# Causal mask by GpSimd's index selection, second-half rotation on GpSimd, and three changes of order, in a two-layer transformer kernel

## The chip, the cores and the metric

The kernel runs on one NeuronCore of a Trainium2 chip. The core has a matrix engine (TensorE, PE in the profile, with its weight loads as PEld), three engines for elementwise work (VectorE or DVE, ScalarE or ACT, GpSimd or POOL) and a queue that only issues transfers (SyncE, SP). Each engine takes its instructions in a fixed order and waits on semaphores that the others raise. The metric is the device time of one execution in microseconds, as the median of several runs.

## The reference

Two layers over 1024 tokens of width 1024, in fp32. Layer 0 mixes tokens by attention in a window of 128 tokens with 16 query heads, 4 key heads and one sink logit a head; layer 1 mixes them by a gated linear recurrence (HGRN2). Each mixer is followed by an MLP with a squared ReLU and 4096 hidden units, and a norm ends it.

```python
def sliding_window_attention(h, positions, w_qkv, b_qkv, sinks, w_o):
    qkv = h @ w_qkv + b_qkv
    q, k = apply_partial_rotary(q, cos, sin), apply_partial_rotary(k, cos, sin)
    scores = einsum(q, band(k)) * HEAD_DIM ** -0.5        # own block of 128 keys and the one before
    mask = (delta >= 0) & (delta < WINDOW) & (key_pos >= 0)
    m = maximum(max(scores), sink); e = exp(where(mask, scores, NEG_INF) - m)
    probs = e / (sum(e) + exp(sink - m))
    return einsum(probs, band(v)) @ w_o
...
for layer in range(DEPTH):
    x = x + mixer(rmsnorm(x, mix_norm[layer]))
    x = x + square(relu(rmsnorm(x, mlp_norm[layer]) @ w_up)) @ w_down
return rmsnorm(x, final_norm)
```

## The kernel before

**How it is written.** The Python code emits operations in program order into a list (`Schedule.add`); a planner then decides, before the kernel is built, which engine runs each one and in what order. Every operation carries a cost in ns for each engine that may run it. `due` (from L146 on) walks the list with a clock that only TensorE's costs advance and gives each operation a due time; an operation emitted with a `lead` is ranked 120 ns earlier for each unit of it. `order` then plays the list through: at each engine's next free moment it takes the ready operation of the lowest rank. All instructions are issued from one line, L372, so the profile is told apart by the tiles' names and not by lines. A cost in the code is therefore not a time: a wrong one moves instructions.

**Numbers in two parts.** Large products run in fp32r, with each operand split into a high and a low part (`wh`, `wl` for weights, two tiles `a` for the other side), and three matmuls of 512 columns stand for one exact one. The splits are made by DVE and ACT.

**Tiles.** `a` are 58 long-lived tiles of 128x512, `t` 20 short-lived ones, `m` 7 for the attention's scores and weight sums, `wr` raw weights as they land, `q` and `p` four banks each of the accumulation memory, `sm` small columns, `c` constants, `d` tiles put by in DRAM.

**Attention** (`attention`). Tokens come in two halves of four blocks of 128. `qkv` of half 0 projects keys and values (column group 0) and two groups of query columns; `projected` adds the bias on DVE and calls `rope`, which rotates 16 of each head's 64 columns with four small DVE operations: two products with the tables of cosine and sine (tiles `c`), one difference, one sum. Then the attention of half 0 is interleaved with the projections of half 1, and the attention of half 1 with the output projection of half 0. The norm's factor `r` of half 1 is asked for at the first step of its projections.

For each key head and block, `attend_block` makes the scores on PE (two `q` banks), copies and masks them into a tile `m` (ACT, DVE), takes the maximum with the sink (DVE; the sink's column is written by POOL), the exponentials (ACT), divides (DVE, `m<-m,sm`) and transposes on PE. A trick folds the window: `m` holds own and previous keys in the same 128 columns, since exactly one of the two is inside the window. ACT copies the transposed weights to `y`; a DVE product of `y` with a mask of zeros and ones (`own`, `t<-t,c` in the profile) keeps those of own keys. `values` then multiplies `y` with the previous block's values and `own` with the difference of the two (PE, `q<-t,a`, 64 columns wide), for two blocks at a time. The first block has no predecessor and takes its mask from the accumulation memory.

**MLP.** The first half works by a Strassen-like scheme on pairs of 128 hidden units (`pair`, m from 0 to 15): seven products of 12 matmuls, named 1 to 7, in three banks. Products 1, 6, 7 and 4 run on in the same bank `main`, and after each of the first three ACT copies the running sum (`read`), before the next product of that bank may begin. Products 5 and 3 share `side`, 2 has `own`. After the last pair comes `down`, the second half of the MLP.

**The recurrence** (`recurrence`) multiplies small pieces, 64 rows by 32 or 64 columns, in true fp32; each is entered to the planner with a cost of `width * 2.06 / 2.4 + 3` ns (L1276). They are interleaved with the projections of other heads.

Of the kernel before, what the change touches and what calls it, by code (L numbers as in the profile page):

```python
# [15 lines left out]
ALU = mybir.AluOpType  # L16
AX = mybir.AxisListType

P = 128
# [6 lines left out]
MT = FF // P  # L26
# [292 lines left out]
class Net:  # L319
# [323 lines left out]
    def pair(self, m, x):  # L643

        w = self.strassen_weights(*(self.io["up"][self.layer, i] for i in (m, m + MT // 2)))

        def read(ps):
            z = self.t()
            self.take(z, ps)
            return z  # L650

        main, side, own = self.psum("q"), self.psum("q"), self.psum()
        self.product(main, w[1], x[1], True)
        u1 = read(main)
        self.product(own, w[2], x[2], True)
        self.product(side, w[5], x[5], True)
        p5 = read(side)
        self.product(main, w[6], x[6], False)
        u2 = read(main)
        self.product(side, w[3], x[3], False)  # L660
        self.product(main, w[7], x[7], False)
        u3 = read(main)
        self.product(main, w[4], x[4], False)
        def kept(name, z):
            self.hid[name, m] = self.keep(z)

        self.add_bank(u1, own)
        h00 = self.square_relu(u1)
        kept(1, h00)
        self.add_bank(u2, side)  # L670
        h01, t5, t6, t4 = self.square_relu(u2), *(self.t() for _ in range(3))
        self.tt("any", t5, h01, h00, ALU.subtract)
        kept(5, t5)
        self.tt("any", p5, p5, u3, ALU.add)
        h11 = self.square_relu(p5)
        kept(3, h11)
        self.tt("any", t6, h11, t5, ALU.subtract)
        kept(6, t6)
        self.tt("any", h01, h11, h01, ALU.subtract)
        kept(7, h01)  # L680
        h10 = self.square_relu(main, True)
        kept(2, h10)
        self.tt("any", t4, h10, t6, ALU.subtract)
        kept(4, t4)
# [188 lines left out]
        self.neg = self.const((P, 1))  # L873
        self.memset(self.neg, NEG)

    def rope(self, x, heads, n):
        half = ROT // 2
        v = x.rearrange("p (h d) -> p h d", d=HD)[:, :, :ROT].rearrange("p h (a r) -> p h a r", a=2)
        prod = []
        for tab in self.trig:  # L880
            y = self.t(F32, (P, 8, 2, half))[:, :heads]
            tb = tab[:, n].unsqueeze(1).unsqueeze(1).to_broadcast([P, heads, 2, half])
            self.tt("any", y, v, tb, ALU.mult, heads * ROT)
            prod.append(y)
        yc, ys = prod
        self.tt("any", v[:, :, 0], yc[:, :, 0], ys[:, :, 1], ALU.subtract, heads * half)
        self.tt("any", v[:, :, 1], yc[:, :, 1], ys[:, :, 0], ALU.add, heads * half)

    def k_tiles(self, i):
        if self.ks[i] is None:  # L890
# [34 lines left out]
    def projected(self, cg, n, ps, r):  # L925
        if cg == 0:
            self.keys_values(n, ps, r)
        else:
            q = self.a()
            self.stt(halves(q), straight(ps), r, halves(self.bias[cg]), ALU.mult, ALU.add)  # L930
            self.rope(q, 8, n)
            self.q[n][cg - 1] = q

    def keys_values(self, n, ps, r):
        W = NG * HD
        k, ps = self.t(F32, (P, W)), straight(ps)
        self.stt(k, ps[:, 0], r, self.bias[0][:, :W], ALU.mult, ALU.add, W)
        if n % 2 == 0:
            self.v.append(self.a(F32, (P, 2, W)))
        v = self.v[n // 2][:, n % 2].only(n)  # L940
        self.stt(v, ps[:, 1], r, self.bias[0][:, W:], ALU.mult, ALU.add, W)
        if n % 2 == 0:
            self.dv.append(self.a(F32, (P, 2, W)))
        if n:
            before = self.v[(n - 1) // 2][:, (n - 1) % 2].only(n - 1)
            self.tt("any", self.dv[n // 2][:, n % 2].only(n), v, before, ALU.subtract, W)
        self.rope(k, NG, n)
        pk = self.psum("q")[:, : 2 * P].rearrange("p (g s) -> p g s", g=2)
        for gp in range(2):
            self.transpose(pk[:, gp], k[:, gp * P : gp * P + P])  # L950
        for i, (first, end) in enumerate(K_SPANS):
            if not first <= n < end:
                continue
            ks, kl = self.k_tiles(i)
            c = slice((n - first) * P, (n - first) * P + P)
            for g in range(NG):
                r, o = self.rows(g)
                src, dst = pk[r, g // 2], ks[g][r, c].only(n)
                self.copy(dst, src, P)
                self.ts("Pool", ks[g][o, c].only(n), dst, 1.0, None, ALU.mult, None, P)  # L960
                self.tt("DVE", kl[g][r, c].only(n), src, dst.bitcast(F32), ALU.subtract, P)
# [41 lines left out]
    def attend_block(self, g, n, stacks):  # L1003
        i = (n >= 3) + (n >= 6)
        c = slice((n - 1 - K_SPANS[i][0]) * P, (n + 1 - K_SPANS[i][0]) * P)
        tok = slice((n % BPH) * P, (n % BPH) * P + P)
        ks, kl = self.ks[i][g].only(n - 1, n), self.kl[i][g].only(n - 1, n, "o")
        m = self.t(F32, (P, 4, P + 2), "m")
        self.ts("Pool", m[:, :, P : P + 1], self.sink[:, 4 * g : 4 * g + 4].unsqueeze(2), 1.0, None, ALU.mult, None, 4)
        scores = [self.psum("q").rearrange("p (h s) -> p h s", h=2) for _ in range(2)]  # L1010
        for h in range(4):
            self.mm(scores[h // 2][:, h % 2], stacks[h][:, tok], turned(ks[:, c]), h % 2 == 0, False, 2 * P)
        for h in range(4):
            self.mm(scores[h // 2][:, h % 2], stacks[h][:, tok], turned(kl[:, c]), False, h % 2 == 1, 2 * P)
        for jj, ps in enumerate(scores):
            mj = m[:, 2 * jj : 2 * jj + 2, :P].only(jj)
            ps = ps.rearrange("p h (s a) -> p h a s", a=2)
            self.copy(mj, ps[:, :, 1], 2 * P)
            prev = ps[:, :, 0] if n else self.neg.unsqueeze(2).to_broadcast([P, 2, P])
            mask = self.prev_mask.unsqueeze(1).to_broadcast([P, 2, P])  # L1020
            self.op("DVE", self.nc.vector.copy_predicated, [mj], [mask, prev], 70 + 2 * P * 1.04, mj, mask, prev)
        mx, den = self.t(F32, (P, 4), "sm"), self.t(F32, (P, 4), "sm")
        self.op("DVE", self.nc.vector.tensor_reduce, [mx], [m], 610, mx, m[:, :, : P + 1], AX.X, ALU.max, negate=True)
        for j in range(4):
            mj = m[:, j, : P + 1].only(f"e{j}")
            self.act(mj, mj, AF.Exp, P, bias=mx[:, j : j + 1], accum=den[:, j : j + 1].only(j))
        self.op("DVE", self.nc.vector.reciprocal, [den], [den], 100, den, den)
        self.tt("any", m[:, :, :P], m[:, :, :P], den.unsqueeze(2).to_broadcast([P, 4, P]), ALU.mult)
        pt = self.psum("q").rearrange("p (h s) -> p h s", h=4)
        for j in range(4):  # L1030
            self.transpose(pt[:, j], m[:, j, :P])
        own, v = self.t(F32, (P, 4, P)), self.v[n // 2].only(n)[:, n % 2, g * HD : g * HD + HD]
        mask = self.own_t.unsqueeze(1).to_broadcast([P, 4, P])
        if n:
            y = self.t(F32, (P, 4, P))
            self.copy(y, pt)
            self.tt("any", own, y, mask, ALU.mult)
            parts = [(y, self.v[(n - 1) // 2].only(n - 1)[:, (n - 1) % 2, g * HD : g * HD + HD]),
                     (own, self.dv[n // 2].only(n)[:, n % 2, g * HD : g * HD + HD])]
        else:  # L1040
            self.tt("DVE", own, pt, mask, ALU.mult)
            parts = [(own, v)]
        return parts
# [15 lines left out]
    def attention(self, layer):  # L1059
# [6 lines left out]
        run(self.qkv(0, *h[0]))  # L1066
        self.load_x([1])
        h.append(self.scaled(layer, 1))
        interleave(self.attend(0, out[0]), self.qkv(1, *h[1]), 16, 24)
        interleave(self.attend(1, out[1]), self.o_proj(0, out[0]), 24, 8)  # L1070
        self.mlp_first(layer)
# [173 lines left out]
    def recurrence(self, e, ready, totals, out):  # L1245
# [23 lines left out]
        def products(part, operands, late, width=CH // 2):  # L1269
            part = part.rearrange("p (c t) -> p c t", c=NC)  # L1270
            for hf, (k, qs) in enumerate(operands):
                for c in range(BPH):
                    for b in range(2):
                        rows = slice(b * CH, b * CH + CH)
                        j = 2 * c + b
                        self.mm(part[rows, hf * BPH + c], chunk(k, j), qs[j], True, True, width, 2.06, "columns", late)  # L1276

        def merge(part, lg):
            H = 1 << lg
# [295 lines left out]
```

## Time and profile before

| | |
|---|---|
| median of 3 runs | 2010.9 us (2010.59 to 2011.6) |
| the profiled execution's own time | 2007.87 us |
| its span, from the first to the last instruction | 2005.5 us |
| granted TensorE clock, mean | 0.998 |
| DVE busy | 1699.2 us, 85% |
| ACT busy | 1013.7 us, 51% |
| POOL busy | 62.7 us, 3%, in 124 instructions |
| moved by DMA | 345.88 MB, mean 172 GB/s |

The page's first part gives each engine's busy time, the second the busy share in 40 slices of the span, the fourth the chain of work that ended last, the fifth the costliest groups of instructions. In the prediction's rows, "us engine line op out<-in" is followed by the tile's size and a count; a bracket at the end of a row of the timeline says how long the engine had been idle and what ended that. A row of the windows gives, for a stretch, its length, then busy time and count of PE, PEld, DVE, ACT and POOL, the clock, the DMA share and GB/s. Matmuls are pipelined: one of 128x512 is shown as 0.38 us long, though the next may start after 0.22.

### The profile page before, as it was taken

To read this page: it belongs to the slowest core of one execution; us is meant where nothing else is said; L and a number is where in the kernel's file an instruction comes from. 1 tells how busy PE (TensorE), PEld (TensorE's weight loads), DVE (VectorE), ACT (ScalarE), POOL (GpSimd) and SP (SyncE) were. 2 spreads that over 40 slices of the span, in tenths; PEclk is the share of its full clock that TensorE was granted. 3 is DMA by queue.
4 is the path that set the end of the run, shared out by engine and by line. 5 is a ranking of instruction groups with operands and counts; after the bars stand their busy time and mean duration, and the time that the engine had idled before them with its cause. 6 is when DMAs were issued, how large, how long until landed. Compare 5 with 4: busy or idle time off the path is not lost.

```text
span 2005.5 us, 32701 instructions
## 1 busy us (share of the span) xinstructions
PE 1979.5 (99%) x11404; PEld 1718.5 (86%) x11404; DVE 1699.2 (85%) x3360; ACT 1013.7 (51%) x2045; POOL 62.7 (3%) x124
## 2 busy tenths in 40 slices
PE   9999999999999999999999999999999999999998
PEld 8877788888888888888888888888888888888887
DVE  8999899777778878799898999989977777887787
ACT  6567796554454323255345555554654445323352
POOL 4030100000000000000000000000000000000001
PEclk9999999999999999999999999999999999999999
DMA  6212463544468967745422212667444446886752
GB/s 216 90 53 59 127 222 120 184 167 160 146 204 292 314 217 264 235 163 176 146 63 78 78 59 90 207 208 244 142 167 160 146 162 237 286 301 215 236 179 85
DMA packets 196677, 345.88 MB, mean 172 GB/s; under 512 B 21536, under 2 KB 31776, under 8 KB 196512
## 3 DMA queue, kind: packets, MB, share of 16 engines
q1 hardware_dynamic: 195936, 343.28, 52.0%
q8 instruction: 89, 1.46, 0.3%
q14 instruction: 76, 0.62, 0.1%
q10 hardware_dynamic: 576, 0.52, 0.1%
HBM read 250.39 MB, written 93.32 MB: 171 GB/s over the span
## 4 chain that ended last, share of the span: by engine, by line
PE 85%; DVE 7%; DMA 3%; issue 2%; ACT 2%; POOL 0%; SPq 0%; POOLq 0%; DVEq 0%; ACTq 0%
PE q L372 51%; PE p L372 34%; DVE t L372 3%; DVE a L372 2%; DVE wl L372 1%; ACT t L372 1%; ACT a L372 1%; DMA wr<-in_down 1%; DVE m L372 0%; DMA a<-in_x 0%; ACT wh L372 0%; ACT m L372 0%; DMA t<-d 0%; DMA wr<-in_wqkv 0%; DMA wr<-in_wv 0%
## 5 line engine op out<-in xcount | busy, mean ns | idle before, releaser
L372 PE MATMUL q<-a,wh 128*128 128x512 f32 x2560 | 761.8, 379 | 3.5 <-ACT t L372 3.5
L372 PE MATMUL p<-a,wh 128*128 128x512 f32 x2112 | 644.6, 383 | 0.1
L372 PEld LDWEIGHTS q<-a,wh 128*128 128x128 f32 x2560 | 482.3, 189 | 74.1 <-ACT t L372 5.0
L372 PE MATMUL q<-a,wl 128*128 128x512 f32 x1280 | 484.9, 379 | 0.0
L372 PEld LDWEIGHTS p<-a,wh 128*128 128x128 f32 x2112 | 394.2, 189 | 54.6 <-issue 1.2
L372 PE MATMUL p<-a,wl 128*128 128x512 f32 x1056 | 401.6, 381 | 0.0
L372 ACT CAST a<-t 128x512 fp32r<-128x512 f32 x283 | 172.0, 619 | 286.0 <-PE q L372 142.8
L372 PEld LDWEIGHTS q<-a,wl 128*128 128x128 f32 x1280 | 241.9, 189 | 34.3
L372 ACT ACTIVATE t<-t 128x512 f32<-128x512 f32 x272 | 171.1, 631 | 189.8 <-DVE t L372 182.2
L372 DVE TENSOR_TENSOR wl<-wr,wh 128x512 fp32r<-128x512 f32 x352 | 240.6, 686 | 11.7 <-ACT wh L372 3.9
L372 DVE TENSOR_TENSOR t<-t,t 128x512 f32<-128x512 f32 (+3 forms) x364 | 224.9, 638 | 26.8 <-ACT t L372 23.1
L372 PEld LDWEIGHTS p<-a,wl 128*128 128x128 f32 x1056 | 199.7, 189 | 26.8 <-issue 0.4
L372 DVE TENSOR_TENSOR a<-t,a 128x512 fp32r<-128x512 f32 (+1 forms) x326 | 217.2, 685 | 6.4 <-ACT a L372 6.0
L372 DVE TENSOR_TENSOR wl<-m,wh 128x512 fp32r<-128x512 f32 x248 | 170.5, 689 | 16.7 <-ACT wh L372 10.1
L372 ACT COPY t<-q 128x512 f32<-128x512 f32 (+2 forms) x214 | 119.4, 560 | 112.6 <-PE q L372 111.5
L372 ACT CAST wh<-wr 128x512 fp32r<-128x512 f32 x173 | 106.5, 618 | 100.2 <-PE p L372 45.7
L372 DVE TENSOR_TENSOR m<-wr,wr 128x512 f32<-128x512 f32 x160 | 110.0, 689 | 39.7 <-DMA wr<-in_down 24.0
L372 DVE CAST wh<-wr 128x512 fp32r<-128x512 f32 x179 | 76.5, 427 | 78.9 <-PE q L372 47.2
L372 ACT CAST wh<-m 128x512 fp32r<-128x512 f32 x154 | 94.8, 618 | 57.2 <-PE q L372 35.1
L372 PE MATMUL p<-wh,a 128*128 128x512 f32 x352 | 110.9, 385 | 0.0
L372 PEld LDWEIGHTS q<-t,t 128*64 128x64 f32 (+1 forms) x2160 | 95.2, 144 | 14.0 <-issue 5.3
L372 PE MATMUL q<-t,t 128*64 128x32 f32 (+2 forms) x2160 | 104.1, 229 | 1.8 <-DVE t L372 1.3
(130 smaller groups left out, 2056.8 us busy)
## 6 DMA issues: line engine op xcount, KB each, us to landing
d<-t SPq DMA_DIRECT2D x276, 256.0 KB, 2.8
t<-d SPq DMA_DIRECT2D x264, 256.0 KB, 4.5
wr<-in_down SPq DMA_DIRECT2D x256, 256.0 KB, 3.9
wr<-in_up SPq DMA_DIRECT2D x128, 256.0 KB, 2.9
a<-d SPq DMA_DIRECT2D x60, 256.0 KB, 5.1
wr<-in_wqkv SPq DMA_DIRECT2D x48, 256.0 KB, 3.0
d<-a SPq DMA_DIRECT2D x48, 256.0 KB, 3.5
wr<-in_win SPq DMA_DIRECT2D x48, 256.0 KB, 2.9
```

The source lines that it names most:

```text
L372: fn(*[place(a) for a in args], **{k: place(v) for k, v in kw.items()})
```

## The change

Five edits. The mask product of `attend_block` goes from DVE to an index selection on GpSimd (`affine_select`), which keeps an element where its key's index is not above its query's and writes zero elsewhere, without a mask tile. The rotation takes its engine as an argument: DVE for keys and for the queries of half 0, GpSimd for the queries of half 1. The factor `r` of half 1 is emitted ahead of the interleaved part, with a lead of 200. The last pair of each MLP (m = 15) takes its products in the order 1, 5, 6, 2, 7, 3, 4; all others keep 1, 2, 5, 6, 3, 7, 4. The planner's cost of the recurrence's small products becomes `width * 3.6 / 2.4 + 3` for 32 columns and `width * 2.4 / 2.4 + 3` for 64. The selection is entered with a cost of 1000 ns.

```diff
         main, side, own = self.psum("q"), self.psum("q"), self.psum()
-        self.product(main, w[1], x[1], True)
-        u1 = read(main)
-        self.product(own, w[2], x[2], True)
-        self.product(side, w[5], x[5], True)
-        p5 = read(side)
-        self.product(main, w[6], x[6], False)
-        u2 = read(main)
-        self.product(side, w[3], x[3], False)
-        self.product(main, w[7], x[7], False)
-        u3 = read(main)
-        self.product(main, w[4], x[4], False)
+        got = {}
+        for name in (1, 5, 6, 2, 7, 3, 4) if m == MT // 2 - 1 else (1, 2, 5, 6, 3, 7, 4):
+            ps = main if name in (1, 6, 7, 4) else own if name == 2 else side
+            self.product(ps, w[name], x[name], name in (1, 2, 5))
+            if name in (1, 5, 6, 7):
+                got[name] = read(ps)
+        u1, p5, u2, u3 = (got[name] for name in (1, 5, 6, 7))
...
-    def rope(self, x, heads, n):
+    def rope(self, x, heads, n, e):
...
-            self.tt("any", y, v, tb, ALU.mult, heads * ROT)
+            self.tt(e, y, v, tb, ALU.mult, heads * ROT)
...
-        self.tt("any", v[:, :, 0], yc[:, :, 0], ys[:, :, 1], ALU.subtract, heads * half)
-        self.tt("any", v[:, :, 1], yc[:, :, 1], ys[:, :, 0], ALU.add, heads * half)
+        self.tt(e, v[:, :, 0], yc[:, :, 0], ys[:, :, 1], ALU.subtract, heads * half)
+        self.tt(e, v[:, :, 1], yc[:, :, 1], ys[:, :, 0], ALU.add, heads * half)
...
-            self.rope(q, 8, n)
+            self.rope(q, 8, n, "DVE" if n < BPH else "Pool")
...
-        self.rope(k, NG, n)
+        self.rope(k, NG, n, "DVE")
...
-            self.tt("any", own, y, mask, ALU.mult)
+            self.op("Pool", self.nc.gpsimd.affine_select, [own], [y], 1000, own, y, [[0, 4], [1, P]], ALU.is_ge, 0.0,
+                    base=0, channel_multiplier=-1)
...
         h.append(self.scaled(layer, 1))
+        self.s.lead = 2 * LEAD
+        r = h[1][1]()
+        self.s.lead = 0
+        h[1] = h[1][0], lambda: r
...
-                        self.mm(part[rows, hf * BPH + c], chunk(k, j), qs[j], True, True, width, 2.06, "columns", late)
+                        self.mm(part[rows, hf * BPH + c], chunk(k, j), qs[j], True, True, width, 3.6 if width < CH else 2.4, "columns", late)
```

What the planner makes of it is seen in the order of the built programs, at three places.

**PE, the end of the last pair of the first MLP.** `q_6780` is the bank `main`; the first row before ends product 7, the last two begin product 4, and `q_7003`, `q_7013` are the first banks of `down`. Before:

```order
L372 MATMUL q_6780<-a_4114,wl_6861 128x512
L372 MATMUL q_7003<-a_6827,wh_6909 128x512
L372 MATMUL q_7003<-a_6841,wh_6909 128x512
L372 MATMUL q_7003<-a_6827,wl_6919 128x512
L372 MATMUL q_7013<-a_6827,wh_6909 128x512
L372 MATMUL q_7013<-a_6841,wh_6909 128x512
L372 MATMUL q_7013<-a_6827,wl_6919 128x512
L372 MATMUL q_6780<-a_4120,wh_6876 128x512
L372 MATMUL q_6780<-a_4219,wh_6876 128x512
```

After, the same place; `q_6839` is now the bank `side`, and these are the last rows of product 7 and the first of product 3, which has twelve.

```order
L372 MATMUL q_6780<-a_4117,wh_6845 128x512
L372 MATMUL q_6780<-a_4209,wh_6845 128x512
L372 MATMUL q_6780<-a_4117,wl_6861 128x512
L372 MATMUL q_6839<-a_3894,wh_6822 128x512
L372 MATMUL q_6839<-a_4156,wh_6822 128x512
L372 MATMUL q_6839<-a_3894,wl_6834 128x512
```

Between products 7 and 4 stood six matmuls of `down`; now the twelve of product 3 stand there, product 4 follows them at once, and the first matmul of `down` comes after product 4.

**ACT at the same place.** The rows run from the copy of `main` after product 6 to the copy after product 7 (`t_7009` before, `t_6978` after), for which product 4 waits. Casts make high parts for `down`; ACTIVATE is the squared ReLU. Before:

```order
L372 COPY t_6940<-q_6780 128x512
L372 CAST a_6952<-t_6921 128x512
L372 CAST a_6962<-t_6929 128x512
L372 CAST wh_6974<-wr_6749 128x512
L372 ACTIVATE t_6989<-t_6940 128x512
L372 ACTIVATE t_6989<-t_6989 128x512
L372 CAST wh_7001<-m_6802 128x512
L372 COPY t_7009<-q_6780 128x512
```

After:

```order
L372 COPY t_6910<-q_6780 128x512
L372 CAST a_6947<-t_6919 128x512
L372 ACTIVATE t_6956<-t_6852 128x512
L372 ACTIVATE t_6956<-t_6956 128x512
L372 CAST wh_6969<-wr_6749 128x512
L372 COPY t_6978<-q_6780 128x512
```

Six operations stood between the two copies, and four do now.

**POOL and DVE in the attention of half 1.** The `m` rows of POOL are the sink's columns; AFFINE_SELECT is the mask of one block; the TENSOR_TENSOR rows begin a rotation. `c_103` on DVE before is the mask of zeros and ones. DVE before:

```order
L372 COPY_PREDICATED m_2105<-c_98,q_2553 128x2x128
L372 TENSOR_TENSOR a_2587<-p_2420,t_2464 128x512
L372 RECIPROCAL sm_2570<-sm_2570 128x4
L372 TENSOR_TENSOR wl_2600<-wr_2235,wh_2520 128x512
L372 TENSOR_TENSOR m_2039<-m_2039,sm_2570 128x4x128
L372 TENSOR_TENSOR t_2619<-t_2602,c_103 128x512
L372 COPY_PREDICATED m_2105<-c_98,q_2596 128x2x128
L372 TENSOR_TENSOR wl_2631<-wr_2284,wh_2530 128x512
L372 TENSOR_REDUCE sm_2642<-m_2105 128x4
L372 TENSOR_TENSOR t_2653<-t_2636,c_103 128x512
```

POOL after:

```order
L372 TENSOR_SCALAR m_2038<-c_337 128x4
L372 AFFINE_SELECT t_2044<-t_2036 128x512
L372 TENSOR_SCALAR m_2101<-c_337 128x4
L372 AFFINE_SELECT t_2110<-t_2099 128x512
L372 TENSOR_SCALAR m_2152<-c_337 128x4
L372 TENSOR_SCALAR m_2257<-c_337 128x4
L372 AFFINE_SELECT t_2269<-t_2260 128x512
L372 TENSOR_SCALAR m_2305<-c_337 128x4
L372 AFFINE_SELECT t_2317<-t_2303 128x512
L372 TENSOR_TENSOR t_2342<-a_2334,c_432 128x128
L372 TENSOR_TENSOR t_2348<-a_2334,c_434 128x128
L372 TENSOR_TENSOR a_2334<-t_2342,t_2348 128x8x8
```

The two products with `c_103` have left DVE; a sink column now has a selection or a rotation ahead of it in POOL's queue.

**PE in the first recurrence.** `q_11851` (before) and `q_11846` (after) are one bank of small products; `p` rows are projections. Before:

```order
L372 MATMUL p_11619<-a_10478,wh_11595 128x512
L372 MATMUL p_11619<-a_10593,wh_11595 128x512
L372 MATMUL p_11619<-a_10478,wl_11602 128x512
L372 MATMUL p_11619<-a_10497,wh_11595 128x512
L372 MATMUL q_11851<-t_11830,t_11818 64x32 x8
L372 MATMUL q_11851<-t_11830,t_11823 64x32 x8
```

After:

```order
L372 MATMUL p_11621<-a_10478,wh_11597 128x512
L372 MATMUL q_11846<-t_11830,t_11818 64x32 x8
L372 MATMUL q_11846<-t_11830,t_11824 64x32 x8
L372 MATMUL q_11846<-t_11727,t_11515 64x32 x8
L372 MATMUL q_11846<-t_11711,t_11584 64x32 x8
L372 MATMUL p_11621<-a_10593,wh_11597 128x512
```

The group of small products has moved three matmuls forward; elsewhere in the recurrence, groups move by one to three matmuls in either direction.

## The prediction

> **What bounds the kernel now.** I read the busy times first, then the stretches, then what PE waits for in them, then the timeline where a wait is long.
>
> ```profile
> PE 1979.5 (99%) x11404; PEld 1718.5 (86%) x11404; DVE 1699.2 (85%) x3360; ACT 1013.7 (51%) x2045; POOL 62.7 (3%) x124
> 75.00:280.00 205.00, 199.37 (x1212) 160.06 (x1212) 186.42 (x424) 151.99 (x488) 25.50 (x49) 1.00 0.29 90
> 320.00:600.00 280.00, 280.00 (x1306) 245.01 (x1305) 216.27 (x394) 144.58 (x251) 0.36 (x2) 1.00 0.48 164
> 1050.00:1340.00 290.00, 287.77 (x2909) 252.45 (x2908) 262.84 (x619) 161.20 (x321) 5.94 (x15) 1.00 0.35 112
> PE q L372 <- DVE a L372: 2.7, 6, 0.7
> PE q L372 <- DVE m L372: 1.7, 2, 1.3
> ```
>
> PE is busy in 1979.5 of 2005.5 us, and no edit removes a matmul, so only PE's idle time, 26.0 us, can be won. The three windows say where it lies. In the attention (75 to 280 us) PE idles 205.00 − 199.37 = 5.63 us, and by the waits of that window 2.7 + 1.7 = 4.4 of it end on DVE, which is busy 186.42 of 205, 91%. In the plain MLP (320 to 600) DVE is at 77% and PE idles not at all. In the first recurrence (1050 to 1340) PE idles 2.23 us with DVE at 91%. So the three places that the edits reach hold little: the attention 5.63, the recurrence 2.23, and the two last pairs, which follow.
>
> **The order of the last pairs.**
>
> ```profile
> 604.37 0.59 PE L372 MATMUL q<-a,wh 128*128 128x512 f32 x2
> 607.09 0.70 PE L372 MATMUL q<-a,wh 128*128 128x512 f32 x2 [1.26 <-ACT t L372]
> 601.62 1.28 ACT L372 CAST a<-t 128x512 fp32r<-128x512 f32 x2 [1.64 <-DMA t<-d]
> 604.76 1.29 ACT L372 ACTIVATE t<-t 128x512 f32<-128x512 f32 x2 [1.34 <-DVE t L372]
> 606.47 0.58 ACT L372 COPY t<-q 128x512 f32<-128x512 f32 x1
> 1693.48 0.59 PE L372 MATMUL q<-a,wh 128*128 128x512 f32 x2
> 1697.19 0.70 PE L372 MATMUL q<-a,wh 128*128 128x512 f32 x2 [2.25 <-ACT t L372]
> 1691.73 1.29 ACT L372 CAST a<-t 128x512 fp32r<-128x512 f32 x2 [2.65 <-DMA t<-d]
> 338.53 15.54 PE q L372 x72
> ```
>
> The last row, of the chain of waits, gives the price of a matmul: 15.54 / 72 = 0.216 us. At 604.37 the six matmuls of `down` start; product 4 starts at 607.09 after 1.26 us of idling, because the ACT copy of 606.47 came late. That copy reads product 7, which was done at about 604.4, but ACT runs in order, and ahead of it stood casts that waited for a DMA until 601.62 and two squared-ReLU steps that waited for DVE until 604.76. The second MLP repeats it with 2.25 us. Together 3.51 us.
>
> After, the twelve matmuls of product 3 stand between 7 and 4. Product 7 ends 12 × 0.216 = 2.6 us earlier, at about 601.8, and product 4 may start at 601.8 + 2.6 = 604.4. ACT has one cast (1.28 / 2 = 0.64), the two steps (1.29), whose sum is that of an earlier product and no longer late, one cast (0.64) and the copy (0.58): 601.62 + 3.15 = 604.8, so a wait of about 0.4 stays. In the second MLP 1691.73 + 3.15 = 1694.9 against 1693.48: 1.4 stays. I take 3.51 − 1.8 = **1.7 us won**. It rests on the same DMA landing; the order moves no transfer ahead of that one, but one that lands 1 us later costs 1 us at product 4. Bounds: 0 (the landing slips as far as the order improves) and 3.5. The six matmuls of `down` now come after product 4, with nothing queued that waits for them sooner.
>
> **The attention.** DVE loses the mask products and half of the rotation.
>
> ```profile
> L372 DVE TENSOR_TENSOR t<-t,c 128x512 f32<-128x512 f32 x28 | 19.3, 688 | 0.5 <-ACT t L372 0.2
> L372 DVE TENSOR_TENSOR t<-a,c 128x128 f32<-128x128 f32 x32 | 8.5, 286 | 0.0
> L372 DVE TENSOR_TENSOR a<-t,t 128x64 f32<-128x64 f32 x32 | 6.8, 219 | 0.2
> ```
>
> 19.3 us of masks go. Of the 32 products and 32 sums of the queries half are those of half 1: 16 × 0.286 + 16 × 0.219 = 8.1 us. DVE falls by 27.4, from 186.42 to 159.0, or 78% of the window: the load under which PE in the MLP never idles. I do not take all 5.63, because some waits are of order and not of load (the first exponentials, below), and because the planner packs a freed engine anew. I take **4.0 won**, somewhat less than the 4.4 that end on DVE. Bounds: 0, and 6.9: all of the idle time, and an estimate of 0.16 more at each of the eight waits, by which a matmul that nothing follows is shown longer (0.38) than its share of a run (0.216).
>
> What POOL takes on is not in the trace at its size; its nearest rows are these.
>
> ```profile
> L372 POOL TENSOR_SCALAR_AFFINE_SELECT c<-t 128x128 f32<-128x128 f32 x1 | 0.3, 292 | 0.1
> L372 POOL TENSOR_SCALAR a<-t 128x512 f32<-128x512 f32 x2 | 3.0, 1525 | 29.9 <-ACT t L372 29.9
> L372 POOL TENSOR_TENSOR a<-a,t 128x256 f32<-128x256 f32 x4 | 2.8, 728 | 20.9 <-ACT t L372 20.9
> 95.25 0.59 ACT L372 COPY t<-q 128x512 f32<-128x512 f32 x1 [1.91 <-PE q L372]
> 95.86 0.69 DVE L372 TENSOR_TENSOR t<-t,c 128x512 f32<-128x512 f32 x1
> 96.90 1.51 PE L372 MATMUL q<-t,a 128*64 128x256 f32 x12
> ```
>
> The same operation on a quarter of the width took 0.292 us. Bounds for 128x512 are 0.292 (all of it fixed cost) and 1.525 (the other POOL operation at that size); I take 4 × 0.292, about 1.1. The last three rows are the path of one selection before: ACT's copy ends at 95.84, the mask product at 96.55, and the twelve matmuls start at 96.90, of which the half that reads `own` comes some 0.9 us in. From the copy's end to that read there are about 97.8 − 95.84 = 2.0 us, and the selection fits with 0.9 to spare; where PE starts the group with `own` the spare is 96.90 − 95.84 − 1.1, nothing. So I cost the selection at nothing, under the cover of the projections that PE has queued ahead of the values; without it, each of the 14 groups waits. A rotation row is 128x128 at most, 0.728 / 2 = 0.36 us, and its 32 rows, under 12 us, are wanted only when the attention of half 1 begins: hidden. Behind a selection or a rotation on POOL stand the sinks' columns, for which the DVE maximum waits; at most 1.1 us late each, and DVE has other blocks' work meanwhile.
>
> ```profile
> 84.79 1.28 ACT L372 ACT_TABLE_LOAD   x1
> 91.85 0.63 PE L372 MATMUL q<-c,m 128*128 128x128 f32 x4 [0.73 <-ACT m L372]
> ```
>
> The factor of half 1 needs a table on ACT, loaded at 84.79 just ahead of the first exponentials, and PE waits 0.73 for those at 91.85. Emitted earlier, that load (1.28) leaves this place; it issues no transfer, but its column work lands on DVE and ACT where the first projections are cleared. I take +0.7 and −0.7: nothing, with bounds of 1 either way.
>
> **The durations.**
>
> ```profile
> 1063.82 1.16 PE L372 MATMUL q<-t,t 128*64 128x32 f32 x32
> 1065.79 0.42 PE L372 MATMUL q<-t,t 128*64 128x32 f32 x6 [0.82 <-DVE t L372]
> ```
>
> A group of 16 products of 32 columns (the trace counts 32, two passes each) took 1.16 us; less about 0.2 for the end of the last one that is 60 ns a product. It was entered with 32 × 2.06 / 2.4 + 3 = 30 ns, and now with 51, so it is nearer the truth. But the group that waits 0.82 us for DVE at 1065.79 now stands three matmuls, 0.65 us, earlier, and PE stands behind it. I take +0.65 there and −0.2 elsewhere: **0.4 lost**; bounds 2.2 either way, the idle time of that window.
>
> **Sum.** −1.7 − 4.0 + 0.4 = −5.3. The profiled execution's own time, 2007.87, becomes 2002.6. The median, 2010.9, stands 3.0 above that execution; on its scale **2005.6 us**.
>
> **The rivals.** *GpSimd and DVE hold each other up.*
>
> ```profile
> 95.30 0.23 POOL L372 TENSOR_SCALAR m<-c 128x4 f32<-128x4 f32 x1 [2.04 <-PE q L372]
> 202.43 1.75 POOL L372 TENSOR_SCALAR m<-c 128x4 f32<-128x4 f32 x1 [16.10 <-DVE sm L372]
> 202.80 0.69 DVE L372 TENSOR_TENSOR m<-m,sm 128x512 f32<-128x512 f32 x1
> 117.08 3.82 POOL L372 TENSOR_SCALAR a<-a 64x128 fp32r<-64x128 f32 x6
> 118.57 0.74 DVE L372 TENSOR_TENSOR wl<-wr,wh 128x512 fp32r<-128x512 f32 x1 [0.26 <-ACT wh L372]
> 1975.54 2.52 POOL L372 TENSOR_TENSOR a<-a,t 128x512 f32<-128x512 f32 x2 [665.42 <-ACT t L372]
> 1977.55 0.79 DVE L372 TENSOR_TENSOR a<-m,a 128x256 f32<-128x256 f32 x1
> L372 DVE TENSOR_TENSOR wl<-wr,wh 128x512 fp32r<-128x512 f32 x43 | 29.4, 683 | 0.4 <-ACT wh L372 0.3
> L372 DVE TENSOR_TENSOR m<-m,sm 128x512 f32<-128x512 f32 x32 | 22.0, 688 | 0.3
> ```
>
> A sink column takes POOL 0.23 us at 95.30, but 1.75 at 202.43, while DVE ran three products of two tiles in a row, one of them at 202.80. At 1977.55 DVE's own product of 256 columns took 0.79 us beside POOL, more than the 0.683 of a product twice as wide. Against it: at 118.57, in the middle of six POOL operations, such a product took 0.74 instead of 0.683. If it holds whenever two such operations meet, POOL's new work, 28 × 1.1 + 32 × 0.36 = 42 us, meets DVE's two-tile products in (29.4 + 22.0) / 159 = 32% of the window by these two groups alone and gives 13.6 of the 27.4 us back: the gain of the attention is halved to −2.0, the sum −3.3, the time **2007.6**. [...] Chance 0.2, since the row against it is the one in which POOL was busiest.
>
> *DVE's time is not what PE waits for.* The planner knows DVE's load; it may spend the freed time on work for later, the selection comes 0.4 us later than the product did, and PE meets as many waits as before. The attention gives 0: 2010.9 − 1.7 + 0.4 = **2009.6**. For it speaks that the eight waits are short, 0.7 and 1.3 us at most, and hang on the place of one operation each; against it the MLP without one. Chance 0.12.
>
> *The selections end late, slower than before.* If the hold of 202.43 (1.75 − 0.23 = 1.5 us) strikes the selections, each takes 1.1 + 1.5 = 2.6 us from the copy, past the cover of 2.0; with the start that the planner has put off by 0.4 for its entry, about 0.8 late on average for each of the 14 groups of values: +11. The attention then gives no gain, and 2010.9 − 1.7 + 0.4 + 11 = **2020**. It decides from a mean hold of 0.9 us on. Against it: DVE's load falls, and chains of three such products get rarer. Chance 0.08.
>
> **How the numbers follow.** Forecast 0.6, rivals 0.2, 0.12 and 0.08. The range: the pairs as taken and the other two terms at their best, −1.7 − 6.9 − 2.2 = −10.8, give 2000.1; no gain in the attention and the pairs with 0.4 lost gives 2011.3. **2000 to 2011.5** leaves out the late selections and a little of each side. A measurement of this kernel can tell 0.2%, 4.0 us, from no change: faster is below 2006.9, which is the forecast; the first two rivals lie within 0.2%, above it. So **faster 0.6, within 0.32, slower 0.08**.
>
> **What would show it.** In the profile after: the DVE row of 28 masks gone, 28 selections on POOL near 1.1 us; DVE near 159 us between 75 and 280 us, and PE idling under 2 us there; at the last pairs waits of product 4 near 0.4 and 1.4; in the recurrence a wait near 1.5 where 0.82 stood. Two-tile products on DVE that average over 0.8 us, or selections far over 1.1, would show the first rival; PE waiting for POOL's `t` in front of the values the last. I am wrong if PE's idle time in the attention stays above 4 us, or if waits appear at a place that no edit touches.

## The result, and the profile after

The changed kernel takes 2033.3 us (median of 4 runs, 2032.14 to 2034.75) against 2010.74 in the same comparison: a ratio of 1.0118, 95% interval 1.010 to 1.0135, or some 23 us slower. Forecast were 5.3 us faster. The first rows are those of the page and the windows that the prediction began with, now of the changed kernel; the last is the row of PE's waits with the largest sum between 1050 and 1345 us.

```profile
PE 1993.0 (98%) x11404; PEld 1726.7 (85%) x11404; DVE 1697.6 (84%) x3328; ACT 998.9 (49%) x2017; POOL 93.5 (5%) x184
75.00:280.00 205.00, 198.07 (x1205) 157.93 (x1204) 178.80 (x384) 148.75 (x485) 56.67 (x109) 1.00 0.31 100
1050.00:1340.00 290.00, 275.83 (x2712) 238.85 (x2710) 251.35 (x583) 147.60 (x290) 6.89 (x16) 0.97 0.31 101
PE q L372 <- DVE t L372: 13.9, 14, 1.7
```

Before, the same row read

```profile
PE q L372 <- DVE t L372: 1.3, 2, 0.8
```

The span grew from 2005.5 to 2030.7 us, 25.2. PE's idle time rose from 26.0 to 2030.7 − 1993.0 = 37.7, by 11.7. Its busy time rose as well, by 13.5, with the same 11404 matmuls. That is seen in the third row: the granted clock, 1.00 in the whole recurrence before, is 0.97. So the loss lies in the recurrence, and it has two parts, waits for DVE and slower matmuls. The attention, where I had put the gain, idles 6.93 us instead of 5.63; the prediction had named over 4 us there as a sign of being wrong.

Below is one group of small products on PE's timeline, the matmuls behind it, and DVE's at the same time.

```profile
1111.57 1.71 PE L372 MATMUL q<-t,t 128*64 128x32 f32 x52
1114.96 0.75 PE L372 MATMUL q<-t,t 128*64 128x32 f32 x12 [1.68 <-DVE t L372]
1116.65 1.06 PE L372 MATMUL p<-a,wh 128*128 128x512 f32 x2
1117.50 0.63 PE L372 MATMUL p<-a,wl 128*128 128x512 f32 x1
1112.19 0.77 DVE L372 COPY_PREDICATED t<-c,q 128x256 f32<-128x256 int32 x1
1114.14 0.76 DVE L372 COPY_PREDICATED t<-c,q 128x256 f32<-128x256 int32 x1
```

After 52 of 64 passes PE stands for 1.68 us, and goes on 0.06 us after the copy of 1114.14 has ended. The same group before ran through, and its copy came after it:

```profile
1106.87 2.06 PE L372 MATMUL q<-t,t 128*64 128x32 f32 x64
1108.97 0.73 DVE L372 COPY_PREDICATED t<-c,q 128x256 f32<-128x256 int32 x1
```

The windows of the same place, cut at the moments at which the clock changes, show the second part.

```profile
1108.31:1111.72 3.41, 3.41 (x22) 2.73 (x20) 3.41 (x9) 2.10 (x5) 0.00 (x0) 1.00 0.00 0
1111.72:1115.13 3.41, 1.73 (x58) 1.62 (x57) 3.41 (x11) 0.97 (x2) 0.56 (x2) 1.00 0.12 34
1115.13:1118.54 3.41, 3.41 (x19) 2.81 (x18) 3.41 (x10) 1.14 (x2) 0.00 (x0) 0.50 0.38 127
1118.54:1121.96 3.42, 3.42 (x17) 2.75 (x15) 1.75 (x5) 2.21 (x5) 0.00 (x0) 1.00 0.00 0
```

PE works 1.73 of 3.41 us in the second stretch, and in the third its clock is halved: 1116.65 to 1117.50 are 0.85 us for two matmuls, 0.43 each instead of 0.216. There are six such stretches between 1020 and 1303 us, all 3.41 us long, each worth 1.7 us (half of 3.41): 10.2 of the 13.5 us of added busy time. The rest, 3.3 us, I did not resolve further.

**What a group waits for.** The order of the built programs says it. A bank `q` takes two levels of 16 products each; the copy of 1114.14 reads the columns of the first level, and the last products write columns of the second. PE's rows for the group above, with the waits, before:

```
L372 MATMUL q_12369<-t_12246,t_12230 64x32 [waits DVE_49]
L372 MATMUL q_12369<-t_12246,t_12230 64x32 x7
```

and after:

```
L372 MATMUL q_12369<-t_12246,t_12230 64x32 [waits DVE_49]
L372 MATMUL q_12369<-t_12246,t_12230 64x32
L372 MATMUL q_12369<-t_12246,t_12230 64x32 [waits DVE_49]
L372 MATMUL q_12369<-t_12246,t_12230 64x32 x5
```

The new wait, in the third row, is for that copy. It was placed ahead of the last six products, and these wait for it, though they write other columns. Of the 16 banks with two levels, 2 are interrupted so before (one is the wait of 0.82 us at 1065.79 in the prediction), and all 16 after. In the trace PE's wait ends with the copy (1114.90 us, and PE goes on at 1114.96); why products for other columns have to wait is not shown, and a run without the wait was not tried.

### The profile page after: what moved, and what is told of

Read it like the earlier page. It is cut to its first block, busy times and chain, and to the rows that moved or that the text cites. A ratio compares the mean times of both kernels' runs of the same rounds, so it can differ in the third digit from the quotient of the medians.

```text
span 2030.7 us, 32703 instructions
## 1 busy us (share of the span) xinstructions
PE 1993.0 (98%) x11404; PEld 1726.7 (85%) x11404; DVE 1697.6 (84%) x3328; ACT 998.9 (49%) x2017; POOL 93.5 (5%) x184
## 4 chain that ended last, share of the span: by engine, by line
PE 84%; DVE 8%; ACT 4%; DMA 2%; issue 2%; SPq 0%; POOL 0%; POOLq 0%; DVEq 0%; ACTq 0%
PE q L372 49%; PE p L372 35%; DVE t L372 4%; ACT t L372 2%; DVE wl L372 1%; DVE m L372 1%; DVE a L372 1%; ACT a L372 1%; DMA t<-d 1%; ACT wh L372 1%; DMA wr<-in_wqkv 0%; DMA t<-v 0%; DMA wr<-in_up 0%; ACT m L372 0%; DVE wh L372 0%
## 5 line engine op out<-in xcount | busy, mean ns | idle before, releaser
L372 PEld LDWEIGHTS p<-a,wh 128*128 128x128 f32 x2112 | 399.2, 191 | 58.5 <-DVE wh L372 1.8
L372 PE MATMUL p<-a,wl 128*128 128x512 f32 x1056 | 406.5, 385 | 0.0
L372 ACT CAST a<-t 128x512 fp32r<-128x512 f32 x277 | 167.8, 618 | 292.4 <-PE q L372 138.8
L372 DVE CAST wh<-wr 128x512 fp32r<-128x512 f32 x198 | 86.2, 435 | 89.6 <-PE q L372 47.0
L372 ACT CAST wh<-wr 128x512 fp32r<-128x512 f32 x154 | 94.8, 618 | 89.3 <-PE p L372 41.8
L372 PE MATMUL q<-t,t 128*64 128x32 f32 (+2 forms) x2160 | 108.4, 230 | 16.1 <-DVE t L372 15.3
```

The lines of the kernel that those rows point to most:

```text
L372: fn(*[place(a) for a in args], **{k: place(v) for k, v in kw.items()})
```

## The experiments

All times are medians. The ratios are to runs of the kernel before on the same chip; three sets ran on three chips, on which the kernel before took 2008.2 to 2008.5 us.

**dur_alone**: the new durations and nothing else.

```diff
-                        self.mm(part[rows, hf * BPH + c], chunk(k, j), qs[j], True, True, width, 2.06, "columns", late)
+                        self.mm(part[rows, hf * BPH + c], chunk(k, j), qs[j], True, True, width, 3.6 if width < CH else 2.4, "columns", late)
```

> The kernel before with the new durations of the recurrence's small products and nothing else. Theory 1 (the durations put each group of small products ahead of the DVE result it needs; PE waits some 14 us there, and in each stretch of 3.41 us that the wait leaves thin, the clock is halved for the next 3.41 us, 1.7 us each time): about 2010.9 + 12 to 14 of waits + 10 of clock = 2033 to 2035, six or so stretches at clock 0.5 between 1000 and 1345 us. Theory 2 (the recurrence is upset by what the attention's edits move ahead of it, the durations being close to harmless as predicted): 2011 to 2012, no stretch at 0.5.

Measured: 2033.0 us, ratio 1.0121 (1.0108 to 1.0134), with six stretches at clock 0.5 before the tail. The waits of 1000 to 1345 us:

```profile
PE q L372 <- DVE t L372: 15.1, 16, 1.7
PE q L372 <- DMA t<-v: 0.6, 2, 0.4
```

**all_but_dur**: the other four edits, with the line above as it was.

> The changed kernel with the old durations, the other four edits kept. Theory 1: the waits of the recurrence fall back to about 2 us, no stretch at clock 0.5 ahead of the tail; with the pairs' 3.5 us won and the attention about 1 us worse, 2007 to 2009. Theory 2: stays above 2028.

Measured: 2007.85 us, 0.9997 (0.9988 to 1.0005), no stretch at 0.5 before the tail. The durations are the whole loss, and theory 2 falls. The other four edits together are worth nothing that these runs can tell.

**dur_read_last** and **after_read_last**: the same edge for the planner (an operation that must be placed before another), on top of the new durations alone and of the whole change.

```diff
-        def merge(part, lg):
+        def merge(part, lg, also=()):
...
-            self.op("DVE", self.nc.vector.copy_predicated, [target], [mask, part], 70 + NC * CH // 2 * 1.04, target, mask, part)
+            self.op("DVE", self.nc.vector.copy_predicated, [target], [mask, part, *also], 70 + NC * CH // 2 * 1.04, target, mask, part)
...
-                merge(low, lg)
+                merge(low, lg, (high,))
```

> The new durations alone, as in dur_alone, and one more edge for the planner: the DVE copy that reads the first half of a group's bank (COPY_PREDICATED t<-c,q) may only be placed after the last product of the second half. In the built programs that copy stands ahead of the group's last products in 2 groups of 32 before and in 16 of 32 with the new durations, and those products then wait for it. Theory 1a (this order is the whole loss; the durations themselves are harmless): waits of 1 to 2 us in the recurrence, no stretch at clock 0.5, 2007 to 2011. Theory 1b (the groups stand too early for their own operands): waits stay near 15 us and the time above 2028.

> The changed kernel, whole, with the same edge. Theory 1a: 2005 to 2009, like all_but_dur, with no stretch at clock 0.5 ahead of the tail. Theory 1b: above 2028.

(Of the 32 banks counted there, 16 hold two levels and can be interrupted.) Measured: 2009.7 us, 1.0010 (1.0001 to 1.0019), and 2009.0 us, 1.0004 (0.9996 to 1.0013). The waits of dur_read_last at 1000 to 1345 us:

```profile
PE q L372 <- DMA t<-v: 2.3, 3, 1.1
PE q L372 <- ACT t L372: 1.0, 2, 0.7
```

The row of 15.1 us is gone, and so are the half-clock stretches of the recurrence. In the built programs of dur_alone and dur_read_last the 16 groups start at the same matmul or at most four apart, so their operands had not been late: 1b falls, and the order of theory 1a is the loss, but for a rest. 1.0010 is not the time of the old durations with the same edge; the comparison of pair_dur_read_last with pair_read_last, below, puts that rest at some 3 in a thousand. So 1a's other half, that the durations themselves are harmless, does not hold.

**dur_filled**: dur_alone with 20 more products in each group of the first two levels, ahead of those that wait.

```diff
...
             for hf, (k, qs) in enumerate(operands):
+                for _ in range(hf * fill):
+                    self.mm(part[CH:, NC - 1], chunk(k, 2 * BPH - 1), qs[2 * BPH - 1], True, True, 0, 0, "columns", late)
...
-                products(high, second, late)
+                products(high, second, late, fill=20 if lg == 1 else 0)
```

> The new durations alone, and in the groups of the first two levels 20 more small products per group (each writes what the group's last product then overwrites), placed three quarters through the group, ahead of the products that wait: 8 x 20 products of about 57 ns, 9 us of work added. If the clock is halved after a stretch of 3.41 us because PE streamed too little in it, the fillers run inside the waits, the half-clock stretches fall from 6 to 2 or fewer and the time falls by 7 to 10 us, to 2023 to 2027, although work was added. If the clock drops for another reason, or the fillers come on top of the waits, the time stays at 2033 or rises to 2042.

Measured: 2051.5 us, 1.0221 (1.0205 to 1.0237). A miss: the fillers came on top.

```profile
1119.33 3.92 PE L372 MATMUL q<-t,t 128*64 128x32 f32 x90
1124.09 0.65 PE L372 MATMUL q<-t,t 128*64 128x32 f32 x14 [0.83 <-DVE t L372]
1123.31 0.72 DVE L372 COPY_PREDICATED t<-c,q 128x256 f32<-128x256 int32 x1 [1.28 <-PE q L372]
```

A filler took 117 ns and not 57 (the fillers all write one half of the bank's rows, where the other products alternate between the halves; that this is the reason is not shown), and DVE's copy waited 1.28 us for a product that PE had behind the fillers: the wait was moved and not filled. 160 fillers of 117 ns are 18.7 us, and the time rose by 18.5 over dur_alone. In the profiled execution the half-clock stretches of the recurrence fell from six to one (of twice the length, 6.8 us). But its mean clock, 0.996, is the highest of the four executions; the other three show 0.992 to 0.994, no more than dur_alone with 0.993 and 0.994. So this run does not show that the fillers kept the clock up, and it gives no price for the clock.

**pair_alone** and **sel_alone**: the change's hunk for the last pair, and its hunk for the mask, each on the kernel before.

```diff
...
+        for name in (1, 5, 6, 2, 7, 3, 4) if m == MT // 2 - 1 else (1, 2, 5, 6, 3, 7, 4):
...
```

> The kernel before with the new order of products in the two last pairs alone. Theory 1: the waits of 1.26 and 2.25 us go, 3.4 us won, about 2007.5, and the recurrence between them stays as it was. Rival: the work that no longer waits meets the next DMA or copy later in the down projection, and the time stays at 2010 to 2011.

```diff
-            self.tt("any", own, y, mask, ALU.mult)
+            self.op("Pool", self.nc.gpsimd.affine_select, [own], [y], 1000, own, y, [[0, 4], [1, P]], ALU.is_ge, 0.0,
+                    base=0, channel_multiplier=-1)
```

> The kernel before with the 28 mask products made by GpSimd's selection, rotation and norm left on DVE and in their old place. The first trace after shows a selection of 0.64 to 1.16 us. If PE's waits in the attention hang on DVE's load, they fall by 2 to 4 us (2007 to 2009). If they hang on single operations' places, they stay at 5 to 7 us (2010 to 2013).

Measured: 2004.7 us, 0.9980 (0.9972 to 0.9989), for the pairs; 2012.3 us, 1.0019 (1.0010 to 1.0028), for the selection. The pairs win about 4 us; the selection loses about as much. Where it does is one place at the end of the attention, here in the timeline and the windows of sel_alone:

```profile
271.34 0.63 PE L372 MATMUL q<-c,m 128*128 128x128 f32 x4 [1.91 <-ACT a L372]
269.87:273.29 3.42, 1.95 (x15) 1.81 (x16) 3.42 (x6) 3.27 (x7) 1.41 (x2) 1.00 0.87 286
273.29:276.70 3.41, 3.41 (x11) 2.19 (x11) 3.41 (x8) 2.79 (x5) 0.21 (x1) 0.50 1.03 385
```

A wait of 1.91 us leaves the stretch with 1.95 us of work, and the next one runs at half clock: 1.9 + 1.7 = 3.6 us. The kernel before has no wait at this place.

**all_but_dur_sel**: pairs, rotation and norm, without the selection.

> Pairs, rotation on GpSimd and the early norm factor; the masks stay on DVE and the durations are the old ones. If the selection alone takes back the pairs' gain (sel_alone: 3.9 us slower), 2004 to 2005, as pair_alone. If rotation or norm take it, near 2008.

Measured: 2008.0 us, 0.9996 (0.9987 to 1.0004). So the selection is not alone in taking back the pairs' gain; without it the same place has a wait of 2.1 us and two half-clock stretches behind it:

```profile
269.67 1.09 PE L372 MATMUL q<-c,m 128*128 128x128 f32 x4 [2.10 <-DVE m L372]
269.65:276.48 6.83, 6.52 (x29) 4.53 (x29) 6.40 (x12) 5.22 (x10) 0.00 (x0) 0.50 1.02 367
```

**pair_read_last**, **norm_pair_read_last**, **pair_dur_read_last**, **sel_cost_745**: the edge with the pairs; with the early norm factor as well; with the new durations instead; and with everything but the durations, the selection entered at its measured cost.

```diff
-            self.op("Pool", self.nc.gpsimd.affine_select, [own], [y], 1000, own, y, [[0, 4], [1, P]], ALU.is_ge, 0.0,
+            self.op("Pool", self.nc.gpsimd.affine_select, [own], [y], 745, own, y, [[0, 4], [1, P]], ALU.is_ge, 0.0,
...
```

> The new order of the last pairs and the edge for the planner, with the old durations and nothing else. The two groups of 32 that are interrupted before (waits of 0.82 and 0.53 us) lose their waits: 1.3 us below pair_alone's 2004.67, about 2003.3. Rival: as in dur_read_last the planner's other order meets late transfers and copies instead, and it stays at 2004 to 2006.

> As pair_read_last, with the early norm factor. The difference between the two is the norm's price: between -1 and +1 us as forecast, and the first exponentials' wait of 0.73 us is gone from PE's waits.

> The kernel before with the new order of the last pairs, the new durations and the edge for the planner, and none of the attention's edits. Theory 1a: at or up to 2 us below pair_alone, 2002 to 2005. If the new durations are worth something in themselves once the copy is kept behind, they show here as the difference from pair_alone.

> The changed kernel with the old durations, the edge, and the selection entered with its measured 745 ns instead of 1000. If the selection loses because the planner puts what follows it too late, this wins 2 to 3 us against all_but_dur (2005 to 2006). If it loses because DVE's freed time is filled with other work and PE's waits hang on single operations, it stays at 2007 to 2009.

Measured, in this order: 2002.5 us, 0.9966 (0.9953 to 0.9980); 2001.6 us, 0.9960 (0.9947 to 0.9974); 2007.8 us, 0.9999 (0.9990 to 1.0008); 2003.7 us, 0.9972 (0.9961 to 0.9982). The first two are the fastest kernels of the study, and the intervals do not tell them apart. With the norm the first exponentials' wait of 0.73 us is gone from the rows, while the waits for DVE's `m` rise from 1.7 to 2.4 us. The third run missed its forecast of 2002 to 2005: even with the copy kept behind, the durations lose 3.3 in a thousand, some 6.6 us (0.9999 against 0.9966 without them, on two chips, the intervals apart). Their order meets transfers and ACT copies instead; those waits of PE, 2.2 and 1.0 us in this run's trace, are about half of it, and the rest is open. The last run contains the edge, worth about 1.4 in a thousand between pair_alone and pair_read_last; it lies 2.5 in a thousand below all_but_dur, so some 2 us would be left for the cost of 745. That is a difference of two comparisons on different chips, and with four intervals of about 1 in a thousand either way it is not clear of nothing. The run's two theories are not told apart.

## Why the prediction was wrong

**The durations: the step that failed.** "I take +0.65 there and −0.2 elsewhere: 0.4 lost; bounds 2.2 either way, the idle time of that window." The runs put 24 us there. Two things were wrong in the step. The bound was one for a gain: idle time limits what can be won, and says nothing on what a new order can lose. And I read only PE's order, where groups move by one to three matmuls, while what decides is on DVE: a copy that moved ahead of the last products of its own bank. A likely reason is that the plan, with 51 instead of 30 ns a product, sees the second level last 0.8 us instead of 0.5, so that the copy, which needs the first level alone, comes free before its end; dur_read_last shows that this order costs the time, not why the planner chose it. That 51 ns are nearer the measured 60 was no protection. The rows showed the case once: the wait of 0.82 us at 1065.79, which I put down to an operand that was late.

**The clock.** The granted clock was 1.00 in every row that I quoted, and no rival let it fall. It added to the loss: 10.2 us of half clock beside 13.9 of waits from 1000 to 1345 us (16.1 against 2.2 before).

**The pairs: mechanism right, gain mis-sized.** Forecast were 1.7 us, bounds 0 and 3.5. ACT of the changed kernel at the first place:

```profile
602.04 0.62 ACT L372 CAST a<-t 128x512 fp32r<-128x512 f32 x1 [3.88 <-DMA t<-d]
602.57 1.29 ACT L372 ACTIVATE t<-t 128x512 f32<-128x512 f32 x2
603.76 0.60 ACT L372 CAST wh<-wr 128x512 fp32r<-128x512 f32 x1
604.27 0.58 ACT L372 COPY t<-q 128x512 f32<-128x512 f32 x1
1720.53 0.70 PE L372 MATMUL q<-a,wh 128*128 128x512 f32 x2 [0.86 <-ACT t L372]
```

Cast, two steps, cast and copy follow each other as worked out, from the DMA's landing to 604.85. PE has no wait here and one of 0.86 us at the second place (last row), against the 0.4 and 1.4 forecast: 3.51 − 0.86 = 2.65 us won in this trace. The runs alone say 0.2% (0.11 to 0.28%), 2 to 6 us.

**The attention: wrong.** Forecast were 4.0 won, bounds 0 and 6.9; the three edits lose about 1.7 in a thousand, 3.4 us, between pair_alone and all_but_dur. These groups of DVE (75 to 280 us) and POOL in the changed kernel show why nothing was won:

```profile
L372 DVE CAST wh<-wr 128x512 fp32r<-128x512 f32 x24 | 11.7, 489 | 6.5 <-PE p L372 4.8 <-DMA wr<-in_wo 1.5
L372 DVE TENSOR_TENSOR wl<-wr,wh 128x512 fp32r<-128x512 f32 x42 | 29.6, 707 | 1.1 <-ACT t L372 0.6
L372 DVE TENSOR_TENSOR m<-m,sm 128x512 f32<-128x512 f32 x32 | 22.8, 713 | 0.4
L372 POOL TENSOR_SCALAR_AFFINE_SELECT t<-t 128x512 f32<-128x512 f32 x28 | 20.8, 745 | 34.6 <-ACT t L372 34.5
L372 POOL TENSOR_TENSOR t<-a,c 128x128 f32<-128x128 f32 x16 | 9.9, 639 | 9.0 <-DVE sm L372 8.1 <-DVE a L372 1.0
```

Before, the first of them read

```profile
L372 DVE CAST wh<-wr 128x512 fp32r<-128x512 f32 x16 | 6.8, 422 | 2.8 <-PE p L372 2.7
```

27.4 us left DVE, but its busy time in the window fell by 7.6 only, from 186.42 to 178.80: the planner filled it with casts and splits that were later or on ACT before (DVE has 24 casts of `wh` where 16 stood, ACT 18 where 27 stood). PE's waits hung on single operations and not on DVE's load, as the second rival said.

That rival's 0 was still too good. In the traces of sel_alone, all_but_dur_sel and after_read_last a wait near 270 us falls into a thin stretch, and the clock is halved behind it (0.50 in the first two, above; a mean of 0.99 between 75 and 320 us in the third). In those of the changed kernel and of all_but_dur it is not (1.00 in both), and PE idles 6.93 us between 75 and 320 us against 6.59 before: those two traces hold next to nothing of the 3.4 us. The mean clock of all executions, 0.9972 in all_but_dur against 0.9981 in pair_alone, would make some 1.8 us of them, an estimate, if half-clock stretches come in some of its executions only (0.995 to 0.999); the rest is open. The norm cost nothing beside the edge (0.9960 against 0.9966), which leaves the rotation as the likely loss of all_but_dur_sel; rotation alone was not run.

**The rivals.** The hold-up of the first rival is there and small: DVE's two-tile products went from 683 and 688 to 707 and 713 ns, 42 × 24 + 32 × 25 ns = 1.8 us in these two groups, where 13.6 were feared. Those of them that ran while POOL worked took 740 and 781 ns on average, the others 683 and 686 as before. Selections took 0.63 us at best, 0.745 on average, where 1.1 were taken. The third rival came nearest in time, 2020, but by luck, through a mechanism that did not occur: PE has no wait for POOL's `t` in the changed kernel.

## What to carry to other kernels

In an order made by a planner, look for each bank or buffer that two parts share: here a read of the first part, placed before the last writes of the second, made the writer wait though the columns differed (13.9 us from 1050 to 1345 us, where 1.3 stood). A better cost for one operation is no improvement by itself; compare the order on the engine that reads, not only on the one that was re-priced. Idle time bounds what a change can win and never what it can lose, and a wait in a stretch in which the matrix engine streams little can cost its own length again in clock: here 1.68 us of wait were followed by 3.41 us at clock 0.50, 1.7 us more.

## What was not expected of the hardware

The clock of TensorE fell to half behind stretches in which PE had worked for half of the time and more: 1.71 to 2.59 of 3.41 us in the six of the changed kernel. I counted, in all fourteen traces, the columns that PE streamed in each stretch of 3.413 us, on the grid that the clock's own changes set (in the changed kernel each half-clock stretch before the tail lasts 3.413 us, and the full-speed ones between them 12, 13 or 26 times that): some 8000 stretches outside start and tail. All 16 falls of the clock there follow stretches with at most 3136 columns, where full speed, 512 in 0.216 us, makes some 8090; 21 others as thin had none behind them, and over 3136 there is no fall. A few matmul records may be missing, so the edge is not sharp. Columns alone do not decide: nine of the 21 are in dur_filled, and in four of those the fillers, 117 ns for 32 columns, kept PE busy for the whole stretch. What does decide is not shown. At 1111.72 PE had a wait of 1.68 us and 1.73 us of work, and the clock fell behind it; at 1156.09 it had 2.45 us of work, and the clock stayed at 1.00.
